# Late conditioning sums moved from GpSimd and ScalarE to VectorE, six unsplit tiles in place of four

## The chip, the cores and the metric

One core of one Trainium2 chip. The metric is the device time of one execution in microseconds (us), the median of several runs. TensorE (PE), VectorE (DVE), ScalarE (ACT), GpSimd (POOL) and SyncE (SP) each work through a queue of their own, in order, and wait for each other through semaphores.

## The reference, cut to what matters

One decoder layer on 256 tokens of width 1024. A conditioning vector c gives six rows of 1024 numbers (shift, scale and gate, for each of two halves):

```python
mod = jax.nn.silu(c) @ w_ada + b_ada
shift1, scale1, gate1, shift2, scale2, gate2 = [m[:, None, :] for m in jnp.split(mod, 6, axis=-1)]
h = rms_norm(x, norm1_w) * (1.0 + scale1) + shift1
proj = h @ w_in        # attention q, k, v; convolution b, c, x; indexer q, k, w
...
x = x + gate1 * (y_mix @ w_out)
h2 = rms_norm(x, norm2_w) * (1.0 + scale2) + shift2
x = x + gate2 * peer_ffn(h2, peer_wq, peer_subkeys, peer_u, peer_v)
```

`y_mix` joins an attention part (an indexer scores the keys, the 64 best of each query are kept, then softmax) and a gated convolution. `peer_ffn` scores 16 heads of keys, picks 16 experts per head and token, and multiplies by the whole tables `peer_u` and `peer_v`. Everything is float32. scale1 and shift1 are needed at the very start; gate1, scale2 and shift2 only at the end of the first half of the layer; gate2 only at the end of the kernel.

## The kernel before, in words

All weights come from memory as tiles of 128 x 1024 floats (512 KB), through one list (`queue`) in one fixed order, each into a `raw` buffer, by transfers that SP issues (L117). After the start of the kernel there are six such buffers in the first half of the layer, used in rotation: the load of the seventh tile from here waits until this one is read for the last time.

A **weight tile** is split by `split` (L121 and L122): ACT writes the rounded part `hi`, DVE the rest `lo`, and the raw buffer is free again. A product is then three fast matmuls (`mm3`, L125 to L127). A tile whose number is in `FULL` is not split: the float32 matmuls of L617 read the raw buffer itself, which stays taken until they are done.

A **conditioning tile** holds 128 x 1024 weights of `w_ada` and is used up on arrival by its function `use`. Three kinds matter here. The early ones (scale1 and shift1, `mod_col`, L232) are one DVE instruction each: product with the row `cr` and sum along the row into one column of `mc`. The late ones of gate1 (`add_row_late`, 8 tiles) are two POOL instructions: raw times one number per partition (L244), then added to `gate1` (L245). The late ones of scale2 and shift2 (`mod_col_late`, 16 tiles) are one POOL product (L238) and one ACT instruction that sums it along the row (L239). Those of gate2 (`add_row`, one DVE instruction, L250) come near the end of the kernel and are not touched.

The list begins with 8 groups of two early conditioning tiles and one tile of the first projection. Then come the weight tiles W, numbered from 0: 0 to 3 attention k, 4 the last of q, 5 to 16 the convolution (c, x and b in turn for each of four blocks), 17 to 20 attention v, 21 to 28 `w_out`; then the tiles of the second half. `ADA_AFTER` says how many late conditioning tiles stand in the list behind which weight tile: one behind each of 0 to 22, two behind 4. They are taken in the order gate1, scale2, shift2.

In the first half the order of the instructions on each engine is that of the program text (`manual_schedule`). It is a loop of one pass for each weight tile n from 0 to 20. A pass takes tile n, runs `fill` until two more tiles are prepared (so the conditioning tile behind n+1 and the split of n+2 are queued here, ahead of everything else of the pass), then issues the matmuls of n, the evictions of tile n-1, and one step of each piece of side work: the indexer's products and sums (`isc`, L417 and L419), the causal mask on POOL (`affine_select`, L424), eight rounds of finding the eight largest (L432, L434), the mask `mb` (L439, L441), the norm of k (L449), and from pass 13 on attention (`attend`: `ml`, L486, L491 and so on). The convolution's evictions on DVE are L599 to L609. Eight passes of `w_out` follow, then `after` (L724, first reader of `gate1`), the second norm, which needs scale2 and shift2, and the second half of the layer.

Of the kernel before, what the change touches and what calls it, by code (L numbers as in the profile page):

```python
# [12 lines left out]
AF = mybir.ActivationFunctionType  # L13
OP = mybir.AluOpType
# [5 lines left out]
KD = D // 128  # L20
# [14 lines left out]


NF = 8
FULL = (6, 9, 12, 15)
KO = (4, 5, 6, 7, 0, 1, 2, 3)
ADA_AFTER = {4: 2, **{n: 1 for n in range(23) if n != 4}}  # L40
MIX = [("c", 0), ("c", 1), ("c", 2), ("c", 3), ("v", 0), ("v", 1)]
STARTS = (0, 6, 7)
LATE = 6
# [52 lines left out]
def body(tc, i, out):  # L96
    nc = tc.nc
# [47 lines left out]
    def advance():  # L145
# [5 lines left out]
        count[0] += 1  # L151
        if count[0] in FULL:
            ahead.append((raw,))
# [29 lines left out]
    sc = keep.tile([128, KD], F32, name="sc")  # L183
# [23 lines left out]
    cr = a1.tile([128, D], F32, name="cr")  # L207
# [11 lines left out]
    gate1 = a1.tile([128, D], F32, name="gate1")  # L219
# [8 lines left out]
    mc = a1.tile([128, 4, KD], F32, name="mc")  # L228

    def mod_col(m, k):  # L230
        def use(raw):
            nc.vector.tensor_tensor_reduce(out=raw, in0=raw, in1=cr, scale=1.0, scalar=0.0,  # L232
                                           op0=OP.mult, op1=OP.add, accum_out=mc[:, m, k:k + 1])
        return use

    def mod_col_late(m, k):
        def use(raw):
            nc.gpsimd.tensor_tensor(raw, raw, cr, op=OP.mult)  # L238
            nc.scalar.activation(out=raw, in_=raw, func=AF.Copy, accum_out=mc[:, m, k:k + 1])  # L239
        return use  # L240

    def add_row_late(acc, k):
        def use(raw):
            nc.gpsimd.tensor_scalar(raw, raw, sc[:, k:k + 1], None, op0=OP.mult)  # L244
            nc.gpsimd.tensor_tensor(acc, acc, raw, op=OP.add)  # L245
        return use

    def add_row(acc, k):
        def use(raw):
            nc.vector.scalar_tensor_tensor(acc, raw, sc[:, k:k + 1], acc, op0=OP.mult, op1=OP.add)  # L250
        return use
# [61 lines left out]
    W += [(i["w_out"][k], None) for k in KO]  # L313
    W += [(i["wq"][hp].rearrange("p k c -> p (k c)"), None) for hp in range(16)]
    W += [(i["pu"][j].rearrange("p k c -> p (k c)"), None) for j in range(NJ)]
    ada = [(i["w_gate"][0, k], add_row_late(gate1, k)) for k in range(KD)]
    ada += [(i["w_mod"][m, k], mod_col_late(m, k)) for m in (2, 3) for k in range(KD)]
    for k in range(KD):
        queue.append((i["w_mod"][0, k], mod_col(0, k)))
        queue.append((i["w_mod"][1, k], mod_col(1, k)))  # L320
        queue.append((i["w_first"][k].rearrange("p n c -> p (n c)"), chunk(k)))
    for n, w in enumerate(W):
        queue.append(w)
        for _ in range(ADA_AFTER.get(n, 0)):
            queue.append(ada.pop(0))
    assert not ada
    for j in range(NJ):
        if j >= 16 and j % 8 == 0 and j < 80:
            k = (j - 16) // 8
# [5 lines left out]
    for tb in range(NT):  # L335
        jk = flat(hT[:, 4 * tb:4 * tb + 4])
        nc.vector.tensor_tensor_reduce(out=jk, in0=xs[:, tb], in1=xs[:, tb], scale=1.0, scalar=0.0,
                                       op0=OP.mult, op1=OP.add, accum_out=xr[:, tb:tb + 1])
# [716 lines left out]
```

## Time and profile before

| | |
|---|---|
| median of 3 runs | 1056.3 us (1052.53 to 1061.11) |
| the profiled execution | 1052.17 us |
| its span in the trace | 1050.4 us |
| PE busy | 1004.7 us (96%) |
| DVE busy | 755.8 us (72%) |
| ACT busy | 608.6 us (58%) |
| POOL busy | 92.2 us (9%) |

Busy times are sums over the whole span, and the span has parts with different limits: the first half of the layer, up to about 216 us, and the long second half. Times of matmuls overlap, since each begins before the one ahead has ended.

### The profile page before, as it was taken

The page shows a single profiled execution, that of the slowest core. Times are in us where ns is not written, and L with a number is a line of the kernel's source. Part 1 is how long each engine was busy: PE and PEld are TensorE (multiplying, and loading weights), DVE is VectorE, ACT ScalarE, POOL GpSimd, SP SyncE. Part 2 cuts the span into 40 slices and gives each one's busy share as a digit, 9 for nine tenths or more (in the row PEclk, how much of TensorE's full clock was granted, in tenths as well). Part 3 has the DMA queues.
Part 4 walks back from the last instruction along what each step waited for, and adds up shares of the span by engine and source line. Part 5 has one row for each costly group of instructions (what it writes and reads, how often), then busy time and mean ns, then how long its engine had stood idle before and what let it go on. Part 6 is the DMA issues. An engine that isn't in the chain of part 4 may idle for free.

```text
span 1050.4 us, 18345 instructions
## 1 busy us (share of the span) xinstructions
PE 1004.7 (96%) x6602; PEld 920.6 (88%) x6602; DVE 755.8 (72%) x2092; ACT 608.6 (58%) x1235; POOL 92.2 (9%) x52
## 2 busy tenths in 40 slices
PE   7984898999999999999999999999999999999998
PEld 6773786899999999999999999998888888888886
DVE  6655864668988899967778888876666666665665
ACT  4442466454544545479988888855455445455543
POOL 1398541000000000000000000000000000000000
PEclk9996888999999999999999999999999999999999
DMA  9944654345555565654444444456767667665663
GB/s 335 357 162 179 241 190 151 101 125 160 175 184 182 181 185 178 183 159 141 141 141 141 140 141 138 139 163 195 216 221 219 216 210 225 206 191 183 191 198 121
DMA packets 52892, 191.82 MB, mean 183 GB/s; under 512 B 6113, under 2 KB 6145, under 8 KB 52674
## 3 DMA queue, kind: packets, MB, share of 16 engines
q1 hardware_dynamic: 52416, 189.30, 56.7%
q8 instruction: 52, 0.85, 0.3%
q10 hardware_dynamic: 146, 1.05, 0.3%
q0 software_dynamic: 240, 0.31, 0.2%
q14 instruction: 38, 0.31, 0.1%
HBM read 189.58 MB, written 1.05 MB: 181 GB/s over the span
## 4 chain that ended last, share of the span: by engine, by line
PE 84%; DVE 4%; POOL 4%; ACT 3%; DMA 3%; issue 2%; ACTq 0%; SPq 0%; POOLq 0%; DVEq 0%
PE mm L125 13%; PE mm L126 13%; PE mm L127 13%; PE acc L127 12%; PE acc L125 12%; PE acc L126 12%; PE pg L968 5%; POOL raw L244 2%; DMA raw<-in_w_mod_dram 2%; POOL gate L245 1%; DVE lo L122 1%; ACT hi L121 1%; PE acc L824 1%; POOL raw L238 1%; ACT ml L491 1%
## 5 line engine op out<-in xcount | busy, mean ns | idle before, releaser
L122 DVE TENSOR_TENSOR lo<-raw,hi 128x1024 fp32r<-128x1024 f32 x297 | 366.2, 1234 | 149.1 <-ACT hi L121 146.7
L121 ACT CAST hi<-raw 128x1024 fp32r<-128x1024 f32 x297 | 310.7, 1047 | 145.4 <-PE mm L126 105.6
L125 PE MATMUL mm<-h2h,hi 128*128 128x256 f32 x1152 | 332.9, 289 | 0.2 <-ACT hi L121 0.2
L126 PE MATMUL mm<-h2l,hi 128*128 128x256 f32 x1152 | 325.8, 283 | 0.0
L127 PE MATMUL mm<-h2h,lo 128*128 128x256 f32 x1152 | 325.7, 283 | 0.0
L125 PEld LDWEIGHTS mm<-h2h,hi 128*128 128x128 f32 x1152 | 220.6, 192 | 0.5 <-ACT hi L121 0.5
L126 PEld LDWEIGHTS mm<-h2l,hi 128*128 128x128 f32 x1152 | 220.9, 192 | 0.0
L127 PEld LDWEIGHTS mm<-h2h,lo 128*128 128x128 f32 x1152 | 220.5, 191 | 0.0
L125 PE MATMUL acc<-hi,wh 128*128 128x512 f32 x512 | 199.6, 390 | 0.0
L126 PE MATMUL acc<-lo,wh 128*128 128x512 f32 x512 | 199.2, 389 | 0.0
L127 PE MATMUL acc<-hi,wl 128*128 128x512 f32 x512 | 199.2, 389 | 0.0
L121 ACT CAST wh<-B 128x256 fp32r<-128x256 f32 x128 | 52.0, 407 | 152.7 <-PE acc L126 151.0
L126 PEld LDWEIGHTS acc<-lo,wh 128*128 128x128 f32 x512 | 96.1, 188 | 20.2 <-issue 0.2
L127 PEld LDWEIGHTS acc<-hi,wl 128*128 128x128 f32 x512 | 96.1, 188 | 20.0
L125 PEld LDWEIGHTS acc<-hi,wh 128*128 128x128 f32 x512 | 96.1, 188 | 20.0 <-issue 0.2
L122 DVE TENSOR_TENSOR wl<-B,wh 128x256 fp32r<-128x256 f32 x128 | 54.3, 425 | 55.5 <-ACT wh L121 54.7
L963 ACT ACTIVATE oi<-iota,Ti 128x128 f32<-128x128 f32 x256 | 88.0, 403 | 0.0
L975 DVE TENSOR_TENSOR B<-pg,B 128x256 f32<-128x256 f32 (+63 forms) x127 | 45.1, 355 | 46.2 <-PE pg L968 46.2
L964 DVE TENSOR_SCALAR oj<-iota,Tj,Tg 128x128 f32<-128x128 f32 x256 | 71.4, 344 | 1.6 <-PE pg L968 1.6
L968 PE MATMUL pg<-oj,oi 128*128 128x128 f32 x512 | 67.6, 275 | 0.0
L968 PEld LDWEIGHTS pg<-oj,oi 128*128 128x128 f32 x512 | 62.9, 192 | 0.0
L910 DVE SCALAR_TENSOR_TENSOR ju<-iota,tf,ce 128x50 f32<-128x50 f32 x256 | 51.9, 271 | 0.0
(223 smaller groups left out, 1035.6 us busy)
## 6 DMA issues: line engine op xcount, KB each, us to landing
raw<-in_pu_dram SPq DMA_DIRECT2D x128, 512.0 KB, 3.6
raw<-in_pv_dram SPq DMA_DIRECT2D x128, 512.0 KB, 4.2
raw<-in_w_mod_dram SPq DMA_DIRECT2D x32, 512.0 KB, 6.5
raw<-in_w_gate_dram SPq DMA_DIRECT2D x16, 512.0 KB, 4.3
raw<-in_wq_dram SPq DMA_DIRECT2D x16, 512.0 KB, 3.7
raw<-in_w_c_dram SPq DMA_DIRECT2D x12, 512.0 KB, 4.3
raw<-in_w_first_dram SPq DMA_DIRECT2D x8, 512.0 KB, 7.0
raw<-in_w_kv_dram SPq DMA_DIRECT2D x8, 512.0 KB, 4.5
```

Source lines behind the costliest of these rows:

```text
L121: nc.scalar.copy(hi, src)
L122: nc.vector.tensor_tensor(lo, src, hi.bitcast(F32), op=OP.subtract)
L125: nc.tensor.matmul(ps, a[0], b[0], start=first, stop=False)
L126: nc.tensor.matmul(ps, a[0], b[1], start=False, stop=False)
L127: nc.tensor.matmul(ps, a[1], b[0], start=False, stop=last)
L238: nc.gpsimd.tensor_tensor(raw, raw, cr, op=OP.mult)
L244: nc.gpsimd.tensor_scalar(raw, raw, sc[:, k:k + 1], None, op0=OP.mult)
L910: nc.vector.scalar_tensor_tensor(ju, iota[:, :NC2], tf[tb][:, h, k:k + 1], ce[tb][:, h], op0=OP.is_equal, op1=OP.mult, accum_out=ef[tb][:, ...
L963: nc.scalar.activation(out=oi[:, n], in_=iota, func=AF.Square, bias=Ti[:, t:t + 1])
L964: nc.vector.tensor_scalar(oj[:, n], iota, Tj[:, t:t + 1], Tg[:, t:t + 1], op0=OP.is_equal, op1=OP.mult)
L968: nc.tensor.matmul(ps[:, n], oi[:, n], oj[:, n], start=True, stop=True)
L975: nc.vector.tensor_tensor(B[:, :m, t], pv[:, j0:j0 + m], B[:, :m, t], op=OP.mult)
```

## The change

All late conditioning tiles are summed on DVE: gate1 by `add_row`, scale2 and shift2 by `mod_col`. The two functions that used POOL and ACT are gone. One conditioning tile stands behind each of the weight tiles 2 to 25 (before: 0 to 22, two behind 4). The unsplit weight tiles are 6, 8, 10, 12, 14 and 16 (before: 6, 9, 12 and 15).

```diff
-FULL = (6, 9, 12, 15)
+FULL = (6, 8, 10, 12, 14, 16)
-ADA_AFTER = {4: 2, **{n: 1 for n in range(23) if n != 4}}
+ADA_AFTER = {n: 1 for n in range(2, 26)}
...
-    def mod_col_late(m, k):
-        def use(raw):
-            nc.gpsimd.tensor_tensor(raw, raw, cr, op=OP.mult)
-            nc.scalar.activation(out=raw, in_=raw, func=AF.Copy, accum_out=mc[:, m, k:k + 1])
-        return use
-
-    def add_row_late(acc, k):
-        def use(raw):
-            nc.gpsimd.tensor_scalar(raw, raw, sc[:, k:k + 1], None, op0=OP.mult)
-            nc.gpsimd.tensor_tensor(acc, acc, raw, op=OP.add)
-        return use
...
-    ada = [(i["w_gate"][0, k], add_row_late(gate1, k)) for k in range(KD)]
-    ada += [(i["w_mod"][m, k], mod_col_late(m, k)) for m in (2, 3) for k in range(KD)]
+    ada = [(i["w_gate"][0, k], add_row(gate1, k)) for k in range(KD)]
+    ada += [(i["w_mod"][m, k], mod_col(m, k)) for m in (2, 3) for k in range(KD)]
```

The two functions that now take all late tiles, unchanged:

```python
    def mod_col(m, k):
        def use(raw):
            nc.vector.tensor_tensor_reduce(out=raw, in0=raw, in1=cr, scale=1.0, scalar=0.0,
                                           op0=OP.mult, op1=OP.add, accum_out=mc[:, m, k:k + 1])
        return use

    def add_row(acc, k):
        def use(raw):
            nc.vector.scalar_tensor_tensor(acc, raw, sc[:, k:k + 1], acc, op0=OP.mult, op1=OP.add)
        return use
```

## Rows read from the trace of the kernel before

**Rows 1.** Windows: start:end, busy us (instructions) by engine, granted clock, DMA share, GB/s.
```profile
43.60:107.30 63.70, 43.02 (x279) 38.14 (x278) 35.09 (x59) 25.66 (x60) 57.40 (x25) 0.84 0.51 180
107.30:156.30 49.00, 41.52 (x270) 37.85 (x269) 36.40 (x94) 28.17 (x60) 26.51 (x12) 0.91 0.65 226
156.30:198.60 42.30, 37.14 (x199) 31.54 (x199) 21.03 (x30) 24.43 (x47) 3.79 (x3) 0.91 0.51 154
...
216.00:1050.40 834.40, 829.70 (x5576) 767.97 (x5576) 622.42 (x1811) 504.52 (x1019) 0.00 (x0) 1.00 0.57 175
```
**Rows 2.** Chain that ended last, in the first half: start us, us, what.
```profile
43.62 3.57 POOL raw L244
...
88.25 2.34 POOL raw L238
...
107.31 3.47 PE acc L617 x16
...
158.36 1.04 ACT raw L239 x2
...
198.61 0.70 DVE tmp L724
```
**Rows 3.** POOL's groups of instructions: count, busy us, mean ns, idle before.
```profile
L238 POOL TENSOR_TENSOR raw<-raw,cr 128x1024 f32<-128x1024 f32 x16 | 41.6, 2600 | 30.7 <-DMA raw<-in_w_mod_dram 28.5 <-ACT hi L121 2.3
L244 POOL TENSOR_SCALAR raw<-raw,sc 128x1024 f32<-128x1024 f32 x8 | 24.7, 3083 | 38.0 <-DMA raw<-in_w_gate_dram 38.0
L245 POOL TENSOR_TENSOR gate<-gate,raw 128x1024 f32<-128x1024 f32 x8 | 19.5, 2436 | 0.7
```
**Rows 4.** Waits, 43 to 200 us: total us, times, longest.
```profile
POOL raw L238 <- DMA raw<-in_w_mod_dram: 28.5, 12, 8.8
...
ACT raw L239 <- POOL up L593: 13.8, 2, 12.4
```
**Rows 5.** Waits of SP's queue, which issues the loads, 43 to 200 us.
```profile
SPq L117 <- POOL gate L245: 35.9, 8, 5.4
...
SPq L117 <- PE acc L617: 5.3, 2, 3.5
```
**Rows 6.** DVE on raw tiles, whole span: ns min/median/max, first and last start.
```profile
L122 DVE TENSOR_TENSOR lo<-raw,hi x297: 1209/1226/2015, 43.2 to 1039.0; 128x1024 fp32r<-128x1024 f32 x149
L232 DVE CUSTOM_DVE_ANT_0 raw<-raw,cr x16: 1218/1226/1227, 10.8 to 39.6; 128x1024 f32<-128x1024 f32 x16
L250 DVE SCALAR_TENSOR_TENSOR gate<-raw,sc,gate x8: 1283/1286/1287, 732.0 to 885.3; 128x1024 f32<-128x1024 f32 x8
```
**Rows 7.** DVE's groups by shape, 0 to 216 us: busy us, mean ns.
```profile
L419 DVE SCALAR_TENSOR_TENSOR isc<-rl,iwt,isc 128x256 f32<-128x256 f32 x7 | 6.3, 904 | 0.0
...
L601 DVE TENSOR_SCALAR yc<-up,cw 128x256 f32<-128x256 f32 x4 | 4.8, 1190 | 0.4
...
L550 DVE SCALAR_TENSOR_TENSOR yml<-yc,cw,ymh 128x256 fp32r<-128x256 f32 x4 | 1.7, 480 | 0.0
```
**Rows 8.** DVE in order of time.
```profile
50.61 1.27 DVE L122 TENSOR_TENSOR lo<-raw,hi 128x1024 fp32r<-128x1024 f32 x1 [3.25 <-ACT hi L121]
...
79.61 3.55 DVE L419 SCALAR_TENSOR_TENSOR isc<-rl,iwt,isc 128x128 f32<-128x128 f32 x4
...
98.40 0.41 DVE L601 TENSOR_SCALAR yc<-up,cw 128x256 f32<-128x256 f32 x1
99.78 0.61 DVE L432 MAX8 mx<-isc 128x8 f32<-128x128 f32 x2
...
156.26 1.23 DVE L122 TENSOR_TENSOR lo<-raw,hi 128x1024 fp32r<-128x1024 f32 x1 [3.63 <-ACT hi L121]
```
**Rows 9.** Chain, 88 to 108 us: one of the split tiles' matmuls.
```profile
106.83 0.12 PE acc L127
```
**Rows 10.** POOL in order of time: the causal mask of the indexer.
```profile
90.58 0.64 POOL L424 TENSOR_SCALAR_AFFINE_SELECT isc<-isc 128x128 f32<-128x128 f32 x2
```
**Rows 11.** DMA issues: KB each, median us from issue to landing.
```profile
raw<-in_w_c_dram SPq DMA_DIRECT2D x12, 512.0 KB, 4.3
```

## The prediction, made before the changed kernel ran

> **What bounds the kernel now.** I read the windows by stage first [rows 1]. From 216 us on PE is busy in 829.7 of 834.4 us at a granted clock of 1.00; nothing of the change works there, so this part moves with its start and keeps its length. The question is the first half. In 43.6 to 107.3 us POOL is busy in 57.4 of 63.7 us while PE, DVE and ACT are at 43.0, 35.1 and 25.7. In 107.3 to 156.3 no engine is full (PE 41.5, DVE 36.4 of 49.0). In 156.3 to 198.6 DVE has 21.0 of 42.3.
>
> Then the chain [rows 2]. It enters POOL at 43.62 and stays on its gate sums, one after the other, until 88.25 + 2.34 = 90.6 us; later POOL's products come up only now and then. POOL's groups give the reason [rows 3]: one gate tile is 3.08 + 2.44 = 5.5 us, and eight of them 44.2 us. The waits show who stands behind POOL [rows 4]: ACT lost 12.4 us at a stretch on its first sum of a late tile, with the splits of the next weight tiles queued behind it. And SP's loads waited 35.9 us in eight waits for a gate sum to free a raw buffer [rows 5]. So in the first of the three stages everything, weight tiles too, comes at POOL's pace.
>
> **The change part by part.** *Removed:* POOL's 41.6 + 24.7 + 19.5 = 85.8 us [rows 3], and ACT's 16 sums. *Added on DVE:* 8 gate tiles at 1.29 us and 16 at 1.23, the times of the same instructions on DVE elsewhere in this trace [rows 6], together 29.9 us; minus two splits (four unsplit tiles become six) at 1.23, 2.5 us. The net is 27.4 us more on DVE.
>
> *What DVE gets back.* Some DVE instructions are stretched while POOL works. The plainest is L601: mean 1.19 us [rows 7], but 0.41 us at 98.40, between two POOL instructions [rows 8]. By that row its group loses 4 x 0.78 = 3.1 us. L419 on 128 x 256 has a mean of 0.90 us where L550, the same operation and size, has 0.48 [rows 7]: 7 x 0.42 = 3.0 us. That is 6.1 us in the two groups that I price, about half in the first stage. The mask products and the norm of k look alike and are left unpriced on purpose; I count 8 us in all, between 6.1 and a bound of 27.4 (all that is added).
>
> The Trainium skill (SBUF — State Buffer, Who interferes with whom) says that a DVE instruction with two SBUF inputs, or in a two-port mode, and a GpSimd instruction that reads SBUF exclude each other, and that whichever comes second waits for the whole of the first. By it the stretch goes entirely with the POOL work; were it DVE's own, it would stay, which is the third rival below.
>
> *Stage 1, to the first matmul of tile 9 (107.31 before [rows 2]).* DVE's work there becomes 35.1 [rows 1] - 4 (half of the 8) + 10.3 (8 gate tiles) - 1.2 (tile 8 is not split) = 40.2 us. Stages 1 and 2 count busy time, and in a row of instructions each begins a little before the last one ends, so 40 is rather high. Idle time stays: DVE waits 3.25 us for its split at 50.61 [rows 8], because ACT empties the first projection's banks first, and that is not touched. But 10.3 us of gate sums want no partner and can start in such gaps, behind the loads. I take 40 us with the one against the other: 63.7 - 40 = **23.7 us gained**. PE has 9 tiles there, at 24 x 0.12 = 2.9 us for a split one [rows 9], and is no bound. With it goes the detour of the indexer: its last sum on DVE ends at 79.61 + 3.55 = 83.2 us, the causal mask stands in POOL's queue behind the gate sums until 90.58 [rows 10], and the first search for maxima comes at 99.78 [rows 8]. With POOL free the mask follows the sum at once.
>
> *Stage 2, to the split of tile 20 (156.26 before [rows 8]).* DVE: 36.4 - 4 + 9 conditioning tiles x 1.23 - 1.2 (seven splits where there were eight) = 42.3 us of 49.0. Here DVE becomes the fullest engine, and what it waits for counts. An unsplit tile keeps its raw buffer until its matmuls are done, so the load of the tile three weight tiles on goes out late. Before, SP waited for such matmuls twice, 5.3 us in all, 3.5 at most [rows 5]. On DVE the split that needs the late load stands in the queue ahead of the evictions, the search for maxima and the attention sums. Four such loads fall in this stage; each can cost between nothing and the 4.3 us from issue to landing [rows 11]. I take 1 us each, nearer to nothing, because the waits before show that only part of them was late: 42.3 + 4 = 46.3, **2.7 us gained**. Two more unsplit tiles cost PE 3.47 [rows 2] - 2.9 = 0.6 us each, which lies under DVE's work.
>
> *Stage 3, to the first reader of gate1 (198.61).* Here one late ACT sum of 1.04 us, with the split behind it, is on the chain at 158.36 [rows 2]; it goes. The last six or so conditioning tiles, 7.4 us, go to a DVE that is idle for 21.3 us of 42.3 [rows 1]. They move behind tiles 23 to 25, in the middle of w_out, whose passes are PE's. If that cover were missing they would cost up to 7.4. **1 us gained.**
>
> *Order of the list.* Conditioning starts two weight tiles later, so SP fetches weight tiles 1 and 2 ahead of the first gate tiles; gate1 is read only much later, and scale2 and shift2 after the last w_out tile. Nothing waits for these shifts. POOL's small work (the zeroing of gate2, its load) only comes earlier.
>
> The sum is 23.7 + 2.7 + 1 = 27.4 us. The profiled execution took 1052.2 us (span 1050.4), so 1024.8; it is 4.1 us under the median, which would give 1028.9. The new profile and the new median may fall either way within the spread of the three runs, so I take 1026.
>
> **The rivals.** *The unsplit tiles starve DVE.* Every second tile unsplit means that five loads wait for matmuls, each for the whole 4.3 us, and the attention work stands behind. That takes 5 x 4.3 - 4 = 17.5 us off the gain: 9.9, or 1042 from the profile and 1046 from the median; about 1043. For it: SP's 3.5 us wait. Against it: DVE, not the matmuls, sets the pace there, so PE is early.
>
> *The stages shrink further.* If the waits on POOL were what spread the second and third stage too, DVE's work alone would be left: stage 2 at 42.3, the further stretch gone down to 36, stage 3 shorter by 5 as conditioning fills gaps. Then another 4 + 6 + 4 = 14 us: 1011 to 1015. For it: PE's clock of 0.84 and 0.91 in these stages [rows 1], which idle stretches go with. Against it: PE is at 41.5 of 49 already.
>
> *The stretch is DVE's own.* The 8 us stay: 1034. The row at 98.40 speaks against it.
>
> *DVE waits where POOL waited: slower.* POOL waited 28.5 us in twelve waits, 2.4 us each, for late tiles to arrive [rows 4], and nobody cared. On DVE each such wait would stand ahead of a split and all that follows. With 24 tiles it costs 57 us against 27.4: about 1082. It decides from 27.4 / 24 = 1.1 us a tile. Against it: the loads came late because POOL and the ACT sums held the raw buffers [rows 5]; now a buffer is free 1.3 us after its tile lands.
>
> *Nothing changes.* The attention chain could have its own length, and the splits merely wait elsewhere. Against it stands POOL's unbroken run on the chain.
>
> **How the numbers follow.** The forecast (gain 18 to 34: 1018 to 1036) has a chance of 0.60; starving by unsplit tiles 0.13 (1036 to 1048); further shrinking 0.17 (1006 to 1018); the stretch that stays 0.04; slower 0.03; no change 0.03. A range of 1010 to 1042 leaves out some 0.06 for the two last, half of the starving case and a third of the shrinking one, which is near 2 in 10. The three runs of before lie within 0.8%, so about 1% is what can be told from no change: under 1045.7 us is faster. That has 0.93, within 1% 0.04, slower 0.03.
>
> **What the profile after would show.** Right: POOL nearly empty after 44 us; the first search for maxima near 78 us instead of 99.78; the matmuls of tile 9 near 84; the split of tile 20 near 130; the first read of gate1 near 171; L601 at 0.4 us throughout; from there to the end the same 852 us. Wrong in stage 2 if DVE's splits wait long for ACT's rounding and that for loads; then SP's waits for the unsplit matmuls have grown. Wrong altogether if DVE's conditioning sums wait for their tiles by over a microsecond each, or if the second half has become longer by itself.

## The result, and the profile after

The changed kernel takes 1025.6 us (median of 4 runs, 1025.3 to 1027.2) against 1057.5 of the kernel before (4 runs, one more than in the table): a ratio of 0.9705, with a 95% interval of 0.9662 to 0.9747. The forecast was 1026, in 1010 to 1042. The medians differ by 31.9 us, the two profiled executions only by 24.9: that of before (1052.2 us) was faster than its four timed runs, that of the changed kernel (1027.2) was its slowest. What follows by stage accounts for the 24.9.

The windows of the changed kernel, cut where the stages of [rows 1] end: the first matmul of tile 9 at 82.3 us, the split of tile 20 at 126.7, the first reader of gate1 at 173.2; then the second half of the layer. The columns are PE, PE's loading of weights, DVE, ACT, POOL, the granted clock, the DMA share and GB/s.

```profile
43.60:82.30 38.70, 38.02 (x267) 33.87 (x266) 32.83 (x69) 21.35 (x53) 1.96 (x4) 0.96 0.75 251
82.30:126.70 44.40, 41.75 (x263) 36.98 (x262) 35.54 (x110) 15.85 (x38) 1.50 (x3) 0.92 0.70 241
126.70:173.20 46.50, 41.65 (x201) 34.95 (x200) 26.62 (x43) 21.45 (x41) 0.00 (x0) 0.82 0.53 176
190.00:1025.50 835.50, 830.46 (x5581) 768.09 (x5579) 621.97 (x1811) 505.76 (x1019) 0.00 (x0) 1.00 0.58 175
```

Stage 1 went from 63.7 to 38.7 us, stage 2 from 49.0 to 44.4, stage 3 from 42.3 to 46.5: 25.0 and 4.6 gained, 4.2 lost. The rest kept its length (851.8 and 852.3 us). That makes the 24.9 us between the two spans, 1050.4 and 1025.5.

What PE waited for shows where most of it came from. The longest ones from 43 to 200 us, before:

```profile
PE mm L454 <- DVE kn L449: 14.8, 1, 14.8
...
PE pg L485 <- DVE mxs L486: 5.0, 1, 5.0
```

and in the changed kernel:

```profile
PE pg L473 <- DVE mxs L474: 2.7, 1, 2.7
PE mm L489 <- ACT sT L491: 2.2, 2, 1.5
PE pg L499 <- ACT vt L566: 1.8, 1, 1.8
```

All of PE's waits in the three stages fall from 33.3 to 8.2 us: in stage 1 from 20.7 to 0.6, in stage 2 from 7.5 to 2.7, in stage 3 from 5.1 to 4.9. The long one of before ended with the norm of k on DVE (L449), which stood in DVE's queue behind a split, whose rounding stood in ACT's behind the late sum that had waited 12.4 us for POOL [rows 4]. PE's busy time fell by 5.0 us in stage 1 and rose by 4.5 in stage 3, where the granted clock went from 0.84 to 0.96 and from 0.91 to 0.82. In stage 1 of the changed kernel PE is busy in 38.02 of 38.70 us and hardly waits: there the pace is PE's now, not DVE's.

The indexer's causal mask on POOL, which began at 90.58 us [rows 10], in order of time:

```profile
69.32 1.81 POOL L412 TENSOR_SCALAR_AFFINE_SELECT isc<-isc 128x128 f32<-128x128 f32 x2 [63.66 <-DVE isc L407]
```

It now follows the last sum on DVE and waits for nothing else. Next, DVE in order of time: the first search for maxima (99.78 us in [rows 8]), an L601 of before (now L589), the split of tile 20 (156.26 in [rows 8]) and the first reader of gate1 (198.61 in [rows 2]).

```profile
75.12 0.41 DVE L589 TENSOR_SCALAR yc<-up,cw 128x256 f32<-128x256 f32 x1
...
76.49 0.61 DVE L420 MAX8 mx<-isc 128x8 f32<-128x128 f32 x2
...
126.67 1.22 DVE L122 TENSOR_TENSOR lo<-raw,hi 128x1024 fp32r<-128x1024 f32 x1 [1.45 <-ACT hi L121]
...
173.18 0.69 DVE L712 TENSOR_TENSOR tmp<-acc,gate 128x512 f32<-128x512 f32 x1 [1.54 <-PE acc L127]
```

Against before these stand 23.3, 29.6 and 25.4 us earlier: the lead grows to tile 20 and then shrinks. DVE's groups by shape show the added work (L232 with its first 16, L238) and the stretch that is gone: L589 was 1190 ns, L407 on 128 x 256 904 ns [rows 7].

```profile
L232 DVE CUSTOM_DVE_ANT_0 raw<-raw,cr 128x1024 f32<-128x1024 f32 x32 | 38.8, 1218 | 5.5 <-DMA raw<-in_w_mod_dram 5.2
...
L238 DVE SCALAR_TENSOR_TENSOR gate<-raw,sc,gate 128x1024 f32<-128x1024 f32 x8 | 10.2, 1271 | 0.0
...
L407 DVE SCALAR_TENSOR_TENSOR isc<-rl,iwt,isc 128x256 f32<-128x256 f32 x7 | 3.3, 477 | 0.0
...
L589 DVE TENSOR_SCALAR yc<-up,cw 128x256 f32<-128x256 f32 x4 | 1.7, 413 | 0.4
```

DVE's added sums waited for nearly no tile (L238 0.0 us, and L232's 5.5 us are those of the start). The waits of SP's queue, which issues the loads, from 43 to 200 us:

```profile
SPq L117 <- DVE lo L122: 36.6, 11, 19.3
SPq L117 <- DVE mc L232: 32.1, 8, 17.1
SPq L117 <- PE acc L605: 25.0, 6, 8.1
...
SPq L117 <- DVE yc L597: 3.7, 2, 2.6
```

The third row answers to L617 in [rows 5]: 5.3 us in two waits have become 25.0 in six, behind the unsplit tiles. The chain, which the trace gives from 74.69 us on, has one late load, that of tile 15:

```profile
91.69 1.14 DVE lo L122
92.85 6.17 DMA raw<-in_w_c_dram
...
99.10 1.05 ACT hi L121
```

It hung on DVE, though: SP's wait just ahead of it is the 2.6 us of the last row above (L597 ends behind that split). By the chain PE's 2.7 us come of this load, but none of the six waits for unsplit matmuls is on the chain.

The loss in stage 3 shows in finer windows of PE's clock. Before, products of attention with v (48 matmuls, the last 40 of them in one piece of the chain) ran at full clock; the changed kernel's windows first, then its chain, then the chain of before:

```profile
138.00:140.00 2.00, 0.79 (x8) 0.66 (x6) 2.00 (x4) 1.29 (x4) 0.00 (x0) 1.00 0.54 104
140.00:142.00 2.00, 1.44 (x13) 1.45 (x13) 1.03 (x3) 1.72 (x4) 0.00 (x0) 1.00 0.98 360
142.00:144.00 2.00, 2.00 (x11) 2.00 (x11) 1.58 (x2) 0.00 (x0) 0.00 (x0) 0.50 0.88 309
...
152.00:154.00 2.00, 2.00 (x6) 1.52 (x6) 0.00 (x0) 0.00 (x0) 0.00 (x0) 0.50 0.00 0
154.00:156.00 2.00, 2.00 (x5) 1.06 (x4) 0.00 (x0) 0.00 (x0) 0.00 (x0) 0.59 0.00 0
156.00:158.00 2.00, 2.00 (x9) 1.30 (x8) 0.24 (x2) 1.67 (x4) 0.00 (x0) 1.00 0.00 0
```

```profile
140.56 7.52 PE pg L499 x40
...
150.70 0.43 PE acc L125
```

```profile
171.47 4.69 PE pg L511 x40
...
178.49 0.23 PE acc L125
```

PE had little to do from 138 to 140.6 us, and from 142 to about 155 us it was granted the lower of its two levels, 1.2 GHz. The same matmuls take 7.52 us instead of 4.69, and the first ones of w_out 0.43 instead of 0.23 us each. From the split of tile 20 to the start of these 40 matmuls stage 3 takes 13.9 us (15.2 before), from there to the first reader of gate1 32.6 (27.1 before): 1.3 gained, 5.5 lost.

### The profile page after: what moved, and what is told of

The parts are those of the page before. It is cut to its first block, busy times and chain, and to the rows that moved or that the text cites. A ratio compares the mean times of both kernels' runs of the same rounds, so it can differ in the third digit from the quotient of the medians.

```text
span 1025.5 us, 18270 instructions
## 1 busy us (share of the span) xinstructions
PE 1004.5 (98%) x6586; PEld 918.4 (90%) x6586; DVE 757.9 (74%) x2130; ACT 590.5 (58%) x1201; POOL 8.1 (1%) x20
## 4 chain that ended last, share of the span: by engine, by line
PE 86%; DVE 3%; ACT 2%; issue 1%; DMA 1%; ACTq 0%; DVEq 0%
PE mm L125 13%; PE mm L126 13%; PE mm L127 13%; PE acc L127 12%; PE acc L126 12%; PE acc L125 12%; PE pg L956 6%; DVE lo L122 1%; PE pg L499 1%; PE acc L812 1%; ACT hi L121 1%; DMA raw<-in_w_c_dram 1%; PE acc L605 1%; DVE raw L232 0%; ACT ml L479 0%
## 5 line engine op out<-in xcount | busy, mean ns | idle before, releaser
L122 DVE TENSOR_TENSOR lo<-raw,hi 128x1024 fp32r<-128x1024 f32 x295 | 360.3, 1222 | 118.0 <-ACT hi L121 115.4
L127 PEld LDWEIGHTS acc<-hi,wl 128*128 128x128 f32 x512 | 96.1, 188 | 20.1
```

The costliest lines, as they stand in the source:

```text
L122: nc.vector.tensor_tensor(lo, src, hi.bitcast(F32), op=OP.subtract)
L127: nc.tensor.matmul(ps, a[1], b[0], start=False, stop=last)
```

## The experiments

All are timed against the kernel before, whose median was 1056.5 to 1057.5 us.

**Which part of the change.** `dve_alone` is the sums on DVE and nothing else, here as an edit of the changed kernel:

```diff
-FULL = (6, 8, 10, 12, 14, 16)
-ADA_AFTER = {n: 1 for n in range(2, 26)}
+FULL = (6, 9, 12, 15)
+ADA_AFTER = {4: 2, **{n: 1 for n in range(23) if n != 4}}
```

> The sums on VectorE, with the old unsplit tiles (6, 9, 12, 15) and the old places in the list (behind tiles 0 to 22). If the gain comes from the POOL work that is gone, as predicted, this kernel has nearly all of it: 1024 to 1031 us, the first search for maxima (L420) near 77 us. If it comes from the new unsplit tiles and places, this kernel stays near the kernel before: 1045 to 1057.

1027.2 us (1025.8 to 1028.0), ratio 0.9719 (0.9688 to 0.9749); first search for maxima at 80.14, 3 us later than expected. The move of the sums alone has all but about 1.5 us of the gain.

`order_alone` is the opposite: those two lines changed in the kernel before, with the sums still on POOL and ACT.

> The new unsplit tiles and the new places in the list, with the late sums still on POOL and ACT. If POOL's pace is the bound of the first stage, nothing is gained: 1050 to 1062 us, the first search for maxima (L432) at 97 to 102 us. If the order brings the gain: 1030 to 1040.

1042.5 us (1039.9 to 1046.8), ratio 0.9874 (0.9832 to 0.9916). Neither number was met: it gains 15 us, with the first search for maxima at 86.31. The prediction's "Nothing waits for these shifts" is wrong for a kernel whose sums are on POOL. Two more runs took it apart, with one of the two lines each.

> The kernel before with nothing changed but the places of the late tiles in the list (behind 2 to 25; sums on POOL and ACT, old unsplit tiles). The run with places and unsplit tiles on POOL reached 1042.5 us where the prediction expected no gain. If the reason is POOL's queue, the places do it alone: the causal mask of the indexer then stands behind six gate sums (82.07 us in that run) and not behind eight gate sums and a product (90.58): 1040 to 1046. If the unsplit tiles did it: 1052 to 1058.

1046.5 us (1042.4 to 1047.0), ratio 0.9888 (0.9848 to 0.9928), just above the first range.

> The kernel before with nothing changed but the unsplit tiles (6, 8, 10, 12, 14, 16). If the places in the list are what helps POOL's kernel: 1052 to 1060, the causal mask still near 90 us. If the unsplit tiles help, because ACT and VectorE split less while they wait for POOL: 1040 to 1047.

1052.9 us (10 runs, 1049.1 to 1060.1), ratio 0.9966 (0.9943 to 0.9989). The places give about 11 us, the unsplit tiles about 4 (barely clear of none), and both about 15. In `places_alone` PE's longest wait, 14.8 us before, is short:

```profile
PE mm L454 <- DVE kn L449: 3.2, 1, 3.2
```

In `unsplit_alone` it is 14.9 us (in two waits), and the causal mask stands at 91.93 us. POOL's queue in `places_alone`:

```profile
75.05 3.84 POOL L244 TENSOR_SCALAR raw<-raw,sc 128x1024 f32<-128x1024 f32 x1
78.98 2.71 POOL L245 TENSOR_TENSOR gate<-gate,raw 128x1024 f32<-128x1024 f32 x1
81.63 0.10 POOL L593 MEMSET up<- 128x2 f32 x1
81.69 1.50 POOL L424 TENSOR_SCALAR_AFFINE_SELECT isc<-isc 128x128 f32<-128x128 f32 x2
83.18 2.84 POOL L244 TENSOR_SCALAR raw<-raw,sc 128x1024 f32<-128x1024 f32 x1
```

The causal mask stands between two gate tiles at 81.69, no longer behind all eight and a product at 90.58 [rows 10]; and fewer sums stand in the list ahead of each weight tile. So POOL's sums still run one after the other, but less of them lies in front. That the shorter wait is all of the 11 us isn't shown: the two profiled executions differ by 6.2 us only (1052.2 and 1046.0).

**Which sums.** With the new order, `gates_dve` has gate1's tiles on DVE, `mods_dve` those of scale2 and shift2; each changes one of two lines:

```diff
-    ada = [(i["w_gate"][0, k], add_row_late(gate1, k)) for k in range(KD)]
-    ada += [(i["w_mod"][m, k], mod_col_late(m, k)) for m in (2, 3) for k in range(KD)]
+    ada = [(i["w_gate"][0, k], add_row(gate1, k)) for k in range(KD)]
+    ada += [(i["w_mod"][m, k], mod_col(m, k)) for m in (2, 3) for k in range(KD)]
```

> The new order, with gate1's 8 tiles on VectorE but the 16 tiles of scale2 and shift2 on POOL and ACT. The prediction puts 23.7 of its 27.4 us in the first stage, where only gate tiles are summed: by it this kernel keeps about 20 us of the gain, 1030 to 1036, and loses some in the second stage to stretched VectorE instructions. If the products on POOL are what counts: 1044 to 1055.

1029.0 us (1026.7 to 1034.0), ratio 0.9747 (0.9704 to 0.9791).

> The new order, with gate1's 8 tiles on POOL (5.5 us each) and the 16 tiles of scale2 and shift2 on VectorE. By the prediction the first stage stays at POOL's pace and the gain is small: 1043 to 1052. If every POOL instruction costs alike (two thirds of the late tiles moved): about 1035.

1034.9 us (1032.4 to 1036.4), ratio 0.9801 (0.9769 to 0.9832). From 1042.5 (`order_alone`) the 8 gate tiles bring 13.5 us, the 16 others 7.6, both 16.8. The gate tiles count most, a tile of them three and a half times as much as one of the others (1.7 us against 0.5), as the prediction had it. `gates_dve` is 1 us faster than expected, and `mods_dve` misses the range of the prediction and meets the figure of the other reading, that every POOL instruction costs alike. By that reading the 8 gate tiles, with half of POOL's 32 instructions on late tiles, would have brought half of the 16.8 us at most; they brought 13.5, so it falls; `mods_dve` started from an order that had gained 15 us where nothing was expected.

**What the stretch of DVE's instructions is worth.** `pool_idle` gives POOL 16 products that hold no buffer:

```diff
+    scr = a1.tile([128, 896], F32, name="scr")
...
+        def use(raw):
+            f(raw)
+            nc.gpsimd.tensor_scalar(scr, cr[:, 0:896], mc[:, m, k:k + 1], None, op0=OP.mult)
```

(`f` is `mod_col(m, k)`.)

> The changed kernel with a POOL product of 896 columns behind each of the 16 scale2 and shift2 sums; it reads an SBUF tile, writes a scratch tile that nobody reads, and no raw buffer waits for it. It prices the stretch alone. If POOL's work stretches VectorE's instructions, as the prediction took it (8 us for 24 tiles and 85.8 us of POOL): L589 and L591 go from 0.41 and 0.49 to about 1 us again, and the time is 1029 to 1036. If the stretch is VectorE's own or lies in its slack: 1023 to 1028.

1026.9 us (1026.3 to 1027.6), ratio 0.9708 (0.9686 to 0.9731): no difference that can be told from the changed kernel. Its second stage in the windows, and the two groups on DVE from 75 to 130 us:

```profile
82.30:126.70 44.40, 42.14 (x275) 37.70 (x274) 39.48 (x110) 17.19 (x43) 29.10 (x13) 0.96 0.72 252
```

```profile
L122 DVE TENSOR_TENSOR lo<-raw,hi 128x1024 fp32r<-128x1024 f32 x8 | 10.9, 1368 | 2.8 <-ACT hi L121 2.8
...
L599 DVE TENSOR_SCALAR yc<-up,cw 128x256 f32<-128x256 f32 x4 | 2.1, 530 | 0.4
```

(The window keeps the bounds of the changed kernel's.) POOL is busy for 29.1 us there, DVE for 39.5 instead of 35.5, with splits of 1368 instead of about 1222 ns and L599 (the L589 of above) at 530 instead of 413. So POOL's work does stretch DVE's, less in this placing than before the change, where L601 had 1190 ns. But the stage is no longer for it: from the first matmul of tile 9 (82.56 us) to the split of tile 20 (125.33) it takes 42.8 us against 44.4. The 3.9 us more on DVE lay in its idle time, and PE's waits in the window are 2.3 us against 2.7. The run doesn't repeat every meeting of the kernel before, so it bounds the price only for POOL work placed like this.

**What the unsplit tiles are worth on DVE.** `full_none` has `FULL = ()`.

> The changed kernel with no unsplit tile at all. VectorE gets six splits more, 7.4 us, ACT 6.3 us; SP no longer waits for unsplit matmuls (25.0 us in six waits in the changed kernel). If VectorE's work is what the second stage consists of: 1027 to 1033. If the late loads behind unsplit tiles cost more than the splits (the rival of starving): 1016 to 1023.

1030.3 us (1028.7 to 1031.5), ratio 0.9737 (0.9712 to 0.9762): 4.7 us slower than the changed kernel. Six splits, on ACT and DVE, cost more than the loads that come late behind unsplit tiles. The rival of starving falls.

**What made stage 3 longer.** `warm_pv` puts 16 spare matmuls into PE's gap ahead of the products with v, `warm_two` 16 more ahead of the transposes of the second block (the two lines under `tb == 1`; the trace shows each 16 as 32):

```diff
-WARM = (20, 18)
+WARM = (20, 18, 16)
...
+        if tb == 1:
+            warm(WARM[2])
         for g in range(2):
             for sb in range(tb + 1):
...
+        if tb == 0:
+            warm(WARM[2])
         po = p_g.tile([128, H, HD], F32, name="pg")
```

> The changed kernel with 16 spare matmuls of ones on PE in the gap of about 1.8 us ahead of the attention-times-v products (L499), results unused. In the changed kernel the granted clock is 0.50 from 142 to 154 us, behind that gap, and L499 takes 7.5 us (4.7 us before the change). If the half clock is what makes the third stage 46.5 us instead of 42.3, and the gap brings it on: clock near 1.00 there, L499 about 4.7 us, 1018 to 1022 us. If the stage is long because VectorE's conditioning sums (136.67 and 139.56) stand ahead of the convolution's rows: 1025 to 1028.

1021.9 us (1019.0 to 1024.0), ratio 0.965 (0.962 to 0.968).

> As warm_pv, with 16 spare matmuls also in the earlier gap of PE, ahead of the second token block's transposes (L489), where the clock of the changed kernel falls to 0.50 for 132 to 135 us. By the clock theory another 1 to 2 us: 1017 to 1021. If one gap is too short to matter, or the matmuls only delay the transposes: no better than warm_pv, or 1 us worse.

1021.1 us (1020.0 to 1022.2), ratio 0.9655 (0.9632 to 0.9678). It is 4.6 us faster than the changed kernel, and no two runs of the two overlap. Windows of 126 to 140 and 140 to 156 us: the changed kernel, `warm_pv`, `warm_two`.

```profile
126.00:140.00 14.00, 10.59 (x76) 10.01 (x74) 8.78 (x13) 10.81 (x23) 0.00 (x0) 0.88 0.64 211
140.00:156.00 16.00, 14.56 (x55) 12.03 (x56) 5.55 (x11) 3.85 (x10) 0.00 (x0) 0.57 0.36 118
```

```profile
126.00:140.00 14.00, 11.79 (x88) 11.35 (x88) 9.57 (x14) 11.17 (x26) 0.00 (x0) 0.88 0.63 226
140.00:156.00 16.00, 14.67 (x83) 12.02 (x82) 6.06 (x12) 5.28 (x11) 0.00 (x0) 0.89 0.29 92
```

```profile
126.00:140.00 14.00, 13.18 (x116) 12.71 (x114) 7.60 (x12) 8.92 (x17) 0.00 (x0) 1.00 0.52 183
140.00:156.00 16.00, 14.68 (x82) 11.78 (x81) 9.51 (x18) 6.46 (x13) 0.00 (x0) 1.00 0.31 97
```

The clock of the second window goes from 0.57 to 0.89 and 1.00 (`warm_two` is some 3.7 us further on in its work there). The split of tile 20 and the first reader of gate1, `warm_pv`, then `warm_two`:

```profile
126.05 1.22 DVE L122 TENSOR_TENSOR lo<-raw,hi 128x1024 fp32r<-128x1024 f32 x1 [1.45 <-ACT hi L121]
170.21 0.69 DVE L714 TENSOR_TENSOR tmp<-acc,gate 128x512 f32<-128x512 f32 x1 [1.54 <-PE acc L127]
```

```profile
123.01 1.23 DVE L122 TENSOR_TENSOR lo<-raw,hi 128x1024 fp32r<-128x1024 f32 x1 [1.45 <-ACT hi L121]
166.29 0.69 DVE L716 TENSOR_TENSOR tmp<-acc,gate 128x512 f32<-128x512 f32 x1 [1.54 <-PE acc L127]
```

Stage 3 is 44.2 and 43.3 us long, instead of 46.5: with the clock kept, 2.3 and 3.2 of the 4.2 us lost are back. The spare matmuls take time of PE themselves, 3.6 us for each set on the chain of `warm_two`. Most of what else parts the profiles of `warm_two` and of the changed kernel, 3.7 us, lies ahead of the split of tile 20, before the first added matmul. Between the two versions no difference can be told.

`warm_late` is `warm_two` with the two sums moved that stood ahead of the convolution's rows in the changed kernel:

```diff
-ADA_AFTER = {n: 1 for n in range(2, 26)}
+ADA_AFTER = {n: 1 for n in range(2, 28) if n not in (21, 22)}
```

> As warm_two, with the conditioning tiles that stood behind weight tiles 21 and 22 moved behind 26 and 27. In the changed kernel these two sums stand on VectorE ahead of the convolution's rows, on the chain at 136.67 us. If they cost something there: 1 to 2 us less than warm_two, 1018.5 to 1020. If the stage is set by PE and ACT once the clock is kept: 1020 to 1022.

1023.0 us (1021.6 to 1026.7), ratio 0.9679 (0.9639 to 0.972): above both ranges, nothing gained. These two sums cost nothing in stage 3 that shows; the others there were not moved. Up to tile 21 this kernel is `warm_two`, and still its profile has the split of tile 20 at 127.06 us, not at 123.01: single executions differ by 4 us ahead of stage 3.

`dve_warm` is `dve_alone` with the spare matmuls of `warm_two`.

> dve_alone (sums on VectorE, old places, old unsplit tiles) with the two sets of 16 spare matmuls of warm_two. The three parts of the change were within 2 us of each other once the sums were on VectorE (1025.6 and 1027.2), though the first search for maxima came 3.7 us later in dve_alone. If the half clock of the third stage hid a real difference, it shows here: 1023 to 1026 against 1021.1 of warm_two. If places and unsplit tiles are worth nothing on VectorE: 1020 to 1022.

1024.5 us (1023.1 to 1025.6), ratio 0.9708 (0.9683 to 0.9734), 3.4 us behind `warm_two`, with intervals that don't overlap. But the expectation's reason is not borne out. Stage 3 is 43.3 us in both profiles, as it is 46.5 in both without the spare matmuls (`dve_alone` and the changed kernel), so the half clock hid no difference there. The 3.3 us between the two lie ahead of tile 20's split (126.33 and 123.01), where `warm_late`, with the places and unsplit tiles of `warm_two`, is about as late as `dve_warm`. What places and unsplit tiles are worth once the sums are on DVE isn't settled: 1.6 us show without spare matmuls (1027.2 against 1025.6), up to 3.4 with them.

## Why the prediction was right, and where its steps were not

*The bound was POOL, in stage 1.* Right: predicted 23.7 us gained there, measured 25.0 in the profiles. The time came from the sums on POOL, as `dve_alone` shows, and from gate1's above all; in stage 1 PE's waits fell by 20.1 us.

*The sum by DVE's work.* Right in its result, wrong in its terms. "I count 8 us in all" was far too little for what DVE gets back. Its busy time in the three stages was 35.1 + 36.4 + 21.0 = 92.5 us and is 32.8 + 35.5 + 26.6 = 94.9: 2.4 more, with 27.4 added, so 25.0 came back. The Trainium skill's rule on the shared interface (SBUF — State Buffer, Who interferes with whom) agrees with that: without POOL's readers L601 went from 1190 to 413 ns and L419 from 904 to 477.

The step that failed is "PE has 9 tiles there, ... and is no bound". It counted nine tiles at 2.9 us, 26 us, and left out the indexer's products (L396), those for the norms (L442, L453), the end of the first projection, and the 5.25 us that tile 8's matmuls took from 77.42 us on (tile 6's took 3.62). PE is busy in 38.0 of stage 1's 38.7 us, with 0.6 us of waits; DVE, by which the stage was summed, has 32.8, where I had 40.2. Stage 2 takes 44.4 us with 35.5 on DVE, where I had 42.3 and waits; PE is at 41.8 there. In each of the two stages some 7 us too much work on DVE and 5 or 6 us too little idle time cancelled, and that the 40 us put down to DVE came out near PE's 38.7 is luck. `pool_idle` shows the same from the other side: 3.9 us of work more on DVE moved nothing. The gain of 27.4 lies between that of the profiles (24.9) and that of the medians (31.9).

*Late loads behind unsplit tiles, 1 us each.* The waits did grow, to 25.0 us on SP's queue, but none is on the chain: the late load there, of tile 15, waited for DVE. That the 4 us of this term are in stage 2 isn't shown; `full_none` shows only that the tiles repay what they cost.

*Stage 3, 1 us gained.* Wrong: 4.2 us lost. Up to the products with v 1.3 us were gained, much as forecast. The step that failed is that the sum kept every length behind that point, and with them PE's clock; there 5.5 us were lost. Before, the granted clock was 1.00 from 168 us on, through the products with v; after, the stage reached them behind a gap and ran 13 us at half clock. `warm_pv` and `warm_two` gain 3.7 and 4.6 us in the medians, 2.3 and 3.2 of it in stage 3 by the profiles. Not all of the rest need come of the spare matmuls: the changed kernel's profile also has a granted clock of 0.51 from 102 to 108 us, and that of `warm_two` has 1.00 there, ahead of every added matmul.

*"Nothing waits for these shifts."* Right of the changed kernel's own queue, wrong as a price: in the kernel with POOL sums the places alone are worth 11 us. It didn't hurt the forecast, since the two reasons overlap: once POOL has no sums, it no longer matters how many of them stand ahead of a tile. Gains of 30 us (sums alone) and 15 us (order alone) make 32 together.

*The rivals.* Starving and slower are out by `full_none` and by the waits of the new sums. That stages shrink further was right for DVE's work and wrong for the time. The stretch is not DVE's own: L601, now L589, is at 413 ns.

## What to carry to other kernels

An engine with few per cent of the span can set the pace of a stage, if raw buffers and in-order steps of others wait for it: read windows by stage, and then who waits for it. Parts of one change that relieve the same queue don't add up; time each alone before crediting one. When waits go, look at what PE's clock does in the gaps that are left: a few spare matmuls there shortened stage 3 by 3.2 us, and that version, 1021.1 us, beats both kernels. And sum a stage for every engine, all its work included: the one that is no bound before can be the bound after.

## What was not expected of the hardware

PE's clock fell to half behind a gap of under 2 us of waiting (1.76 us ahead of 140.56, with a thin stretch before it) and stayed there for some 13 us, although PE was busy throughout all but one of the windows of 2 us from 142 us on. The stages of before already stood at 0.84 and 0.91 [rows 1]. In stage 3 of before the clock was at 0.50 from 162 to 166 us, but back at 1.00 ahead of the products with v, and a thin window behind them left it there:

```profile
176.00:178.00 2.00, 0.67 (x5) 0.24 (x4) 1.81 (x5) 0.76 (x2) 0.00 (x0) 1.00 0.77 236
178.00:180.00 2.00, 2.00 (x9) 1.65 (x10) 1.13 (x3) 1.38 (x5) 0.00 (x0) 1.00 0.06 25
```

So not every thin stretch brings the clock down; which ones do isn't shown.

POOL's own times vary too: a product of 896 columns in `pool_idle` took 3.07 us in the mean, where the same operation on 1024 columns took 2.84 us at best in the kernel before and 3.82 at most. Whether DVE holds POOL up in its turn was not tried.
